# The MLP's gate and up projections in seven block products, with two weight sums made by accumulating transfers

## The chip, the cores and the metric

The kernel runs on one core of a Trainium2 chip. The metric is the device time of one execution, in microseconds (us). A core has five engines that run their own instruction streams in order: TensorE (PE in the profile) multiplies matrices into PSUM, VectorE (DVE) and ScalarE (ACT) work on tiles, GpSimd (POOL) does a little of the same, and SyncE (SP) issues transfers between the chip's memory and SBUF. An instruction that waits holds up everything behind it on its engine.

## The reference

One decoder layer on 512 tokens of width 1024, in float32: two kinds of attention side by side, an output projection added to the input, and then

```
hn = rms_norm(h, norm2_g)
h  = h + (silu(hn @ w_gate) * (hn @ w_up)) @ w_down      # w_gate, w_up: 1024 x 2816, w_down: 2816 x 1024
return rms_norm(h, norm_f_g)
```

## The kernel before

A float32 product is made from three matmuls of rounded halves: each operand is split into hi (a rounded copy, a CAST) and lo (what is left, a subtraction), and `mm3` adds hi·hi, hi·lo and lo·hi into one PSUM bank. So each weight tile that arrives (`w_raw`, 128x512) costs a CAST on ScalarE and a subtraction on VectorE or GpSimd (`split`, which makes `w_hl`) before TensorE can use it.

The work of interest has four stages. Attention ends with `finish_pair`, which puts the last pair's output into `act_hi` on ScalarE and `act_lo` on GpSimd. The second half of the output projection follows (`w_o[f, :, 512:1024]` for f = 0 to 7): the bank is added to the first half's sum (`hp`, kept in memory) to give `h1`, which is scaled and split into `Xh` and `Xl` and turned into `h1t` for the norm. Then gate and up: for each of 22 units j of 128 hidden columns, `gate_up` makes two banks of 128x512 with 8 x 3 matmuls each, and `swiglu` joins them. The norm's factor per token (`R2`) is applied to the results, not to X. Last, down: two passes of 22 steps with four token tiles each, the final norm and the stores.

The instructions of each engine are ordered by a scheduler when the program is built; a buffer that is used again makes the new writer wait for the old readers. The tile pool `ws` that holds `w_raw` and `w_hl` lives through the whole program, while pool `ff`, which takes the space of the attention's pool, opens after attention: its tiles wait until what lay there is no longer used.

Of the kernel before, what the change touches and what calls it, by code (L numbers as in the profile page):

```python
# [16 lines left out]
P = 128  # L17
S = 512
# [20 lines left out]
BUFS = {"w_raw": 3, "w_hl": 5, "pf": 2, "P": 2, "T": 2, "mf": 1, "oc": 1, "g": 4, "h1": 5, "pair": 1}  # L39
ENG = {"0": "apav", "ob": "ap", "s": "vvvp", "w": "avap", "m": "vp", "o0": "av", "b0": "vpvp", "v0": "vv", "r0":  # L40
# [12 lines left out]
def tile_hybrid_layer(ctx: ExitStack, tc: tile.TileContext, xT, w_qk0, w_t, w_av, w_vb, w_o, w_gu, w_d,  # L53
# [5 lines left out]
    ws = ctx.enter_context(tc.tile_pool(name="ws", bufs=2))  # L59
# [27 lines left out]
    def mm3(ps, w, sl, xh, xl, first, last):  # L87

        nc.tensor.matmul(ps, w[:, 0, sl], xh, start=first, stop=False)  # L89
        nc.tensor.matmul(ps, w[:, 0, sl], xl, start=False, stop=False)  # L90
        nc.tensor.matmul(ps, w[:, 1, sl], xh, start=False, stop=last)  # L91
# [47 lines left out]

    ph1 = ExitStack()  # L140
# [161 lines left out]
    mixh = act.tile([P, KT, S], F32R, name="act_hi")  # L302
    mixl = act.tile([P, KT, S], F32R, name="act_lo")
# [73 lines left out]
    def blocks(i, wi, tok):  # L377

        f = scaled(proj_t(i, tok), 1.0, MISC["tr"])
        r = at.tile([P, 2, S], F32, name="Qb", bufs=2)  # L380
        nb = S - CSTRIDE
        for g in range(2):
            gp = slice(64 * g, 64 * g + 64)
            nc.gpsimd.memset(r[64:128, g, nb:], 0.0)
            for h, n in ((0, S), (1, nb)):
                hp = slice(64 * h, 64 * h + 64)
                nc.vector.tensor_tensor(out=r[hp, g, :n].rearrange("p (n l) -> p n l", l=CSTRIDE),
                                        in0=f[gp, S - n:].rearrange("p (n l) -> p n l", l=CSTRIDE), op=ALU.add,
                                        in1=pos_sb[gp, None, h].to_broadcast([64, n // CSTRIDE, CSTRIDE]))
        rhl = (mixh if wi == 0 else mixl)[:, 4:8].rearrange("p (x g) s -> p x g s", x=2)  # L390
# [244 lines left out]


    Gh = [act.tile([P, KT, S], F32R, name=n) for n in ("act_hi", "act_lo")]
    G6 = ff.tile([P, 2 * NJ - 2 * KT, S], F32R, name="G6", bufs=1)
    slots = [Gh[i // KT][:, i % KT] for i in range(2 * KT)] + [G6[:, i] for i in range(2 * NJ - 2 * KT)]
    GH, GL = slots[:NJ], slots[NJ:]  # L640
    TAGS = ("S", "proj", "PT", "S", "proj", "PT", "PT")

    def gate_up(j, a):
        ps = bank(TAGS[(2 * j + a) % len(TAGS)])
        for c in range(2):
            w = split(w_gu[j, a, :, c * WC:(c + 1) * WC], WC, *ENG["gu"][2 * c:2 * c + 2])
            for k in range(4):
                kt = 4 * c + k
                mm3(ps, w, slice(k * P, (k + 1) * P), Xh[:, kt], Xl[:, kt], kt == 0, kt == KT - 1)
        return ps  # L650

    def swiglu(j, pg, pu):
        z = ff.tile([P, S], F32, name="g", bufs=BUFS["g"])
        tt("v", z, pg, R2, ALU.mult)
        nc.scalar.activation(z, z, AF.Silu)
        tt(ENG["h"][0], z, z, R2, ALU.mult)
        tt("v", z, pu, z, ALU.mult)
        copy(ENG["h"][1], GH[j], z)
        tt(ENG["h"][2], GL[j], z, GH[j].bitcast(F32), ALU.subtract)
# [29 lines left out]

    def combine(ps, t, c):  # L690
        tt("v", cell(t, c), ps[t], cell(t, c), ALU.add)
        square(t, c)
        if c == 0:
            tt(ENG["c"], cell(t, 0), cell(t, 0), gf[:, :HD], ALU.mult)
        else:
            finish(t)

    held = None
    for c in range(2):
        ps = [bank(n) for n in (("S", "S", "proj", "proj"), ("PT", "PT", "PT", "O"))[c]]  # L700
        for k in range(NJ - LAST):
            w = w_down(k, c)
            for t in range(NT):
                down(ps, t, k, w)
            if held and k in (1, 3, 5, 7):
                combine(held, k // 2, 0)
        ws_last = [w_down(k, c) for k in range(NJ - LAST, NJ)]
        for t in range(NT):
            for i, k in enumerate(range(NJ - LAST, NJ)):
                down(ps, t, k, ws_last[i])  # L710
            if c == 1:
                combine(ps, t, 1)
        held = ps
# [78 lines left out]
```

## Time and profile before

| | |
|---|---|
| median of 3 runs (lowest to highest) | 682.05 us (680.85 to 682.81) |
| profiled execution, its own time | 679.24 us |
| its span, first to last instruction | 677.5 us |
| mean granted TensorE clock | 0.986 of full speed |
| TensorE matmul busy | 657.1 us (97%) |
| VectorE, ScalarE, GpSimd busy | 381.5, 305.5, 143.8 us |

The time of an execution is its span and 1.7 us around it. A busy time counts an engine's instructions; matmuls overlap each other in the records, so how fast TensorE goes is read from the distance of their starts. "Granted clock" is the share of full TensorE speed (2.4 GHz) that was allowed in a stretch; 0.5 would be the lower level, 1.2 GHz.

### The profile page before, as it was taken

The numbers are of one execution on the slowest core, as the hardware profiler recorded it, in microseconds if no ns is written. First come the engines' busy times: TensorE is split into PE (matmuls) and PEld (weight loads), VectorE is DVE, ScalarE is ACT, GpSimd is POOL, SyncE is SP. The second block draws the span as 40 slices with busy tenths as digits, with TensorE's granted clock in tenths as the row PEclk, the third lists the DMA queues.
The fourth block names the chain that finished last, engine by engine and source line by source line (L and its number), as shares of the span: only waits on it lengthen the run. The fifth ranks groups of instructions, "written<-read, shape, count | busy, mean of one in ns | idle before, by whom it ended". The sixth has DMA issues, their size and how long they took to land.

```text
span 677.5 us, 9409 instructions
## 1 busy us (share of the span) xinstructions
PE 657.1 (97%) x3150; PEld 547.0 (81%) x3150; DVE 381.5 (56%) x828; ACT 305.5 (45%) x668; POOL 143.8 (21%) x184
## 2 busy tenths in 40 slices
PE   9999997999999999899999999999999999999995
PEld 6888897888878887778888888888888888888884
DVE  4468776777877679484645555445445532243225
ACT  5544565436765678466433333333333322232214
POOL 6635842253355455320000000000000000000000
PEclk9999998989999999999999999999999999999998
DMA  6766666445236640062222222222223232213213
GB/s 187 225 172 187 174 171 162 126 138 160 79 110 167 208 121 5 1 228 83 94 94 104 98 94 94 100 103 93 94 94 104 98 124 94 93 66 120 94 48 124
DMA packets 47180, 80.13 MB, mean 118 GB/s; under 512 B 7019, under 2 KB 10347, under 8 KB 47132
## 3 DMA queue, kind: packets, MB, share of 16 engines
q1 hardware_dynamic: 46556, 78.48, 37.2%
q10 hardware_dynamic: 576, 1.05, 0.4%
q8 instruction: 25, 0.41, 0.3%
q14 instruction: 23, 0.19, 0.1%
HBM read 66.36 MB, written 5.55 MB: 106 GB/s over the span
## 4 chain that ended last, share of the span: by engine, by line
PE 92%; DVE 3%; ACT 2%; DMA 1%; issue 1%; SPq 0%; ACTq 0%; DVEq 0%
PE proj L89 9%; PE proj L90 9%; PE proj L91 9%; PE PT L89 5%; PE PT L90 5%; PE PT L91 5%; PE S L89 4%; PE S L90 4%; PE S L91 4%; PE PT L340 3%; PE proj L96 2%; PE proj L95 2%; PE proj L97 2%; PE PT L96 2%; PE PT L95 2%; PE PT L97 2%
## 5 line engine op out<-in xcount | busy, mean ns | idle before, releaser
L71 ACT CAST w_hl<-w_raw 128x512 fp32r<-128x512 f32 (+2 forms) x187 | 112.2, 603 | 261.5 <-PE PT L91 62.9
L84 DVE TENSOR_TENSOR w_hl<-w_raw,w_hl 128x512 fp32r<-128x512 f32 (+1 forms) x169 | 116.9, 693 | 145.1 <-ACT w_hl L71 144.6
L84 POOL TENSOR_TENSOR w_hl<-w_raw,w_hl 128x512 fp32r<-128x512 f32 (+1 forms) x47 | 60.9, 1301 | 63.5 <-ACT w_hl L71 26.1
L337 POOL TENSOR_SCALAR P<-P,den 128x512 f32<-128x512 f32 (+1 forms) x96 | 51.5, 558 | 39.1 <-DVE den L329 27.4
L325 ACT ACTIVATE P<-P,mn 128x512 f32<-128x512 f32 (+1 forms) x96 | 53.5, 559 | 12.7 <-DVE mn L323 12.5
L89 PE MATMUL PT<-Xh,w_hl 128*128 128x512 f32 x144 | 56.0, 389 | 0.0
L90 PE MATMUL PT<-Xl,w_hl 128*128 128x512 f32 x144 | 56.0, 389 | 0.0
L91 PE MATMUL PT<-Xh,w_hl 128*128 128x512 f32 x144 | 56.0, 389 | 0.0
L76 DVE TENSOR_TENSOR PTl<-PT,PTh 128x512 fp32r<-128x512 f32 (+2 forms) x96 | 43.8, 482 | 9.7 <-ACT PTh L350 9.3
L323 DVE CUSTOM_DVE_ANT_0 P<-S,T 128x512 f32<-128x512 f32 (+1 forms) x96 | 44.0, 483 | 8.6 <-PE S L318 7.1
L350 ACT CAST PTh<-PT 128x512 fp32r<-128x512 f32 (+2 forms) x96 | 38.1, 426 | 22.3 <-PE PT L340 18.3
L89 PE MATMUL proj<-xh,w_hl 128*128 128x512 f32 x112 | 45.9, 410 | 0.0
L90 PE MATMUL proj<-xl,w_hl 128*128 128x512 f32 x112 | 45.2, 403 | 0.0
L91 PE MATMUL proj<-xh,w_hl 128*128 128x512 f32 x112 | 45.1, 403 | 0.0
L91 PE MATMUL S<-Xh,w_hl 128*128 128x512 f32 x104 | 40.9, 393 | 0.0
L89 PE MATMUL S<-Xh,w_hl 128*128 128x512 f32 x104 | 40.7, 392 | 0.0
L90 PE MATMUL S<-Xl,w_hl 128*128 128x512 f32 x104 | 40.5, 389 | 0.0
L89 PE MATMUL proj<-Xh,w_hl 128*128 128x512 f32 x104 | 40.5, 389 | 0.0
L90 PE MATMUL proj<-Xl,w_hl 128*128 128x512 f32 x104 | 40.5, 389 | 0.0
L91 PE MATMUL proj<-Xh,w_hl 128*128 128x512 f32 x104 | 40.5, 389 | 0.0
L340 PE MATMUL PT<-ident,P 128*128 128x128 f32 x240 | 36.0, 273 | 0.8 <-POOL P L337 0.8
L340 PEld LDWEIGHTS PT<-ident,P 128*128 128x128 f32 x240 | 28.3, 140 | 5.1 <-POOL P L337 1.3
(275 smaller groups left out, 1423.4 us busy)
## 6 DMA issues: line engine op xcount, KB each, us to landing
w_raw<-in_w_gu_dram SPq DMA_DIRECT2D x88, 256.0 KB, 2.7
w_raw<-in_w_d_dram SPq DMA_DIRECT2D x44, 256.0 KB, 2.8
w_raw<-in_w_t_dram SPq DMA_DIRECT2D x28, 256.0 KB, 2.9
T<-gd SPq DMA_DIRECT2D x64, 64.0 KB, 2.0
w_raw<-in_w_o_dram SPq DMA_DIRECT2D x16, 256.0 KB, 3.0
w_raw<-in_w_vb_dram SPq DMA_DIRECT2D x16, 140.0 KB, 2.2
Qb<-in_xT_dram SPq DMA_DIRECT2D x8, 256.0 KB, 3.0
w_raw<-in_w_av_dram SPq DMA_DIRECT2D x8, 256.0 KB, 2.8
```

The lines of the kernel that those rows point to most:

```text
L71: nc.scalar.copy(out, in_)
L76: engines[e].tensor_tensor(out=out, in0=in0, in1=in1, op=op)
L84: engines[lo].tensor_tensor(out=w[:, 1, :n], in0=raw[:, :n], in1=w[:, 0, :n].bitcast(F32), op=ALU.subtract)
L89: nc.tensor.matmul(ps, w[:, 0, sl], xh, start=first, stop=False)
L90: nc.tensor.matmul(ps, w[:, 0, sl], xl, start=False, stop=False)
L91: nc.tensor.matmul(ps, w[:, 1, sl], xh, start=False, stop=last)
L95: nc.tensor.matmul(ps, xh, w[:, 0, sl], start=first, stop=False)
L323: nc.vector.tensor_tensor_reduce(out=pp, in0=sv, in1=T[:, S - w:], op0=ALU.add, op1=ALU.min, scale=1.0, scalar=3e38, accum_out=mn[:, t:t + 1])
L325: nc.scalar.activation(pp, pp, AF.Exp, bias=mn[:, t:t + 1], scale=-1.0, accum_out=den[:, t:t + 1])
L337: nc.gpsimd.tensor_scalar(pp, pp, den[:, t:t + 1], 1.0, op0=ALU.mult, op1=ALU.mult)
L340: nc.tensor.transpose(pv[:, kb * P:(kb + 1) * P], pp[:, kb * P:(kb + 1) * P], ident)
L350: nc.scalar.copy(ov[0], pv)
```

## The change

The gate and up weights of a unit, cut into first and second 512 inputs, are four blocks: a and b of gate, c and d of up. The tokens are cut into two halves of 256. The eight block products that make the unit's gate and up (each over 512 inputs, 256 tokens) become seven products of sums of blocks: a, b, d, S1 = c + d, S2 = S1 + a, S3 = c + a and S4 = S2 + b, each with its own sum of blocks of X. Each product is 4 x 3 matmuls of 256 columns, so a unit has 84 matmuls of 256 columns where it had 48 of 512. The results are put together with three copies on ScalarE (`q1`, `p5`, `u2`) and adds on VectorE.

Weights are loaded into double tiles (`raw2`, 128x1024, split in one CAST and one subtraction into `hl2`); d has tiles of its own (`raw1`, `hl1`). S1 and S3 are made by transfers: c is loaded by SP, and GpSimd then issues a transfer of d (for S1) or a (for S3) that adds to the same tile. S2 and S4 are additions on VectorE. So seven transfers of 256 KB a unit take the place of four.

X is made in `lower` and `upper`: two blocks of the first 512 inputs (`X1`) and five of the second (`X2`), sums made on VectorE and then split in hi and lo. The output projection's second half takes pairs of f, with loads from pool `ff` (the pool `ws` now closes with attention). z and y of the units stay in float32 and are split in the down stage, which makes one pass with all eight banks; `h1t` goes to memory (`h1d`) and comes back at the end. The act tiles are cut in four.

```
-BUFS = {"w_raw": 3, "w_hl": 5, ..., "g": 4, "h1": 5, "pair": 1}
+BUFS = {"w_raw": 3, "w_hl": 5, ..., "g": 2, "h1": 4, "pair": 1, "raw2": 5, "raw1": 3,
+        "hl2": 3, "hl1": 2, "xe": 2, "xf": 1, "q": 6, "y": 2}
+SUMS = "d"
-ENG = {..., "ob": "ap", ...}
+ENG = {..., "ob": "pvpv", ...}
...
+    def lower(k):
+        e = ff.tile([P, 3, HS], F32, name="xe", bufs=BUFS["xe"])
+        nc.scalar.activation(e[:, 0:3:2], h1s[k].rearrange("p (a n) -> p a n", a=2), AF.Copy, scale=ng[:, k:k + 1])
+        tt("v", e[:, 1], e[:, 0], e[:, 2], ALU.subtract)
+        copy("a", X1[0][:, k], e[:, 0:2])
+        tt("v", X1[1][:, k], e[:, 0:2], X1[0][:, k].bitcast(F32), ALU.subtract)
+        return e
+    def upper(k, e):
+        f = ff.tile([P, 5, HS], F32, name="xf", bufs=BUFS["xf"])
...
+        copy("a", X2[0][:, k], f)
+        tt("v", X2[1][:, k], f, X2[0][:, k].bitcast(F32), ALU.subtract)
+    for k in range(HK):
+        raw = raw2()
+        for n, f in enumerate((k, HK + k)):
+            nc.sync.dma_start(raw[:, n], w_o[f, :, 512:1024])
+        w = split2(raw, "a", ENG["ob"][k])
...
+    def weights(j):
+        l0, l1, l2, d = raw2(), raw2(), raw2(), raw1()
+        nc.sync.dma_start(l0[:, 0], w_gu[j, 0, :, 0:WC])
+        nc.sync.dma_start(d, w_gu[j, 1, :, WC:])
+        nc.sync.dma_start(l1[:, 1], w_gu[j, 0, :, WC:])
+        if SUMS == "d":
+            nc.sync.dma_start(l0[:, 1], w_gu[j, 1, :, 0:WC])
+            nc.gpsimd.dma_start(l0[:, 1], w_gu[j, 1, :, WC:], accum_op=ALU.add)
+            nc.sync.dma_start(l2[:, 1], w_gu[j, 1, :, 0:WC])
+            nc.gpsimd.dma_start(l2[:, 1], w_gu[j, 0, :, 0:WC], accum_op=ALU.add)
...
+        w0 = split2(l0, "a", "v")
+        tt("v", l1[:, 0], l0[:, 1], l0[:, 0], ALU.add)
+        w1 = split2(l1, "a", "v")
+        tt("v", l2[:, 0], l1[:, 0], l1[:, 1], ALU.add)
...
+        w2 = split2(l2, "a", "v")
+        wd = split1(d, "a", "v")
+    def product(ps, w, X, b, first):
+        for k in range(HK):
+            mm3(ps, w, slice(k * P, (k + 1) * P), X[0][:, k, b], X[1][:, k, b], first and k == 0, k == HK - 1, True)
-    for j in range(NJ):
-        pg = gate_up(j, 0)
-        if j == 0:
-            second_norm()
-        pu = gate_up(j, 1)
-        swiglu(j, pg, pu)
+    for j in range(NJ):
+        now = first_part(j)
+        if j == 0:
+            second_norm()
+        else:
+            third_part(j - 1, before)
+        second_part(j, now)
+        before = now
+    third_part(NJ - 1, before)
```

`first_part` does the products a and S1, `second_part` S2, b, S4 and S3, `third_part` d.

How the rows stand on VectorE in the middle of gate and up, before, for about one unit and a half (`w_hl` is a lo, the other rows are `swiglu`):

```order
L76 TENSOR_TENSOR g_4300<-S_4265,g_4300 128x512
L84 TENSOR_TENSOR w_hl_4387<-w_raw_4385,w_hl_4387 128x512
L76 TENSOR_TENSOR G6_3573<-g_4300,act_lo_3572 128x512
L84 TENSOR_TENSOR w_hl_4404<-w_raw_4402,w_hl_4404 128x512
L76 TENSOR_TENSOR g_4377<-proj_4307,R2_3570 128x512
L84 TENSOR_TENSOR w_hl_4422<-w_raw_4420,w_hl_4422 128x512
L76 TENSOR_TENSOR g_4377<-g_4377,R2_3570 128x512
L84 TENSOR_TENSOR w_hl_4439<-w_raw_4437,w_hl_4439 128x512
L76 TENSOR_TENSOR g_4377<-PT_4342,g_4377 128x512
L84 TENSOR_TENSOR w_hl_4464<-w_raw_4462,w_hl_4464 128x512
L76 TENSOR_TENSOR G6_3573<-g_4377,act_lo_3572 128x512
L84 TENSOR_TENSOR w_hl_4481<-w_raw_4479,w_hl_4481 128x512
```

After, one unit's length of VectorE's rows, with the tile numbers: `raw2_4387`, `raw2_4388` and `raw2_4389` are l0, l1 and l2 of unit 6, `raw2_4261`, `raw2_4262`, `raw2_4263` those of unit 5, and `raw2_4136` is l1 of unit 4 (the rows begin with S2 of unit 5; the next row behind them is `raw2_4388<-raw2_4387`, S2 of unit 6):

```order
L77 TENSOR_TENSOR raw2_4262<-raw2_4261 128x512
L77 TENSOR_TENSOR hl1_4157<-raw1_4138,hl1_4157 128x512
L77 TENSOR_TENSOR raw2_4263<-raw2_4262 128x512
L77 TENSOR_TENSOR y_4037<-proj_4036,q_4040 128x256
L77 TENSOR_TENSOR hl2_4150<-raw2_4136,hl2_4150 128x1024
L77 TENSOR_TENSOR y_4037<-y_4037,R2_3594 128x512
L77 TENSOR_TENSOR act00_3595<-S_4034,q_4039 128x256
L77 TENSOR_TENSOR act00_3595<-act00_3595,y_4037 128x256
L77 TENSOR_TENSOR hl2_4154<-raw2_4137,hl2_4154 128x1024
L77 TENSOR_TENSOR y_4163<-PT_4161,q_4164 128x256
L77 TENSOR_TENSOR hl2_4272<-raw2_4261,hl2_4272 128x1024
L77 TENSOR_TENSOR act00_3595<-S_4034,y_4037 128x256
```

A unit's four lo subtractions of 512 have become three of 1024 (`hl2`) and one of 512 (`hl1`), with two sums into `raw2` between them. S2 is the first reader of what the accumulating transfer leaves in l0. The tile `raw2_4387` lies where `raw2_4136` lay (there are five such buffers), whose last reader is the fifth row, `hl2_4150<-raw2_4136`.

The transfers of unit 6 on SP, after (L699 is a, L703 the load of c into l0, L701 b, L705 the load of c into l2, L700 a later unit's d; the first waits for that fifth row):

```order
L699 DMA raw2_4387<-in_w_gu_dram 128x512
L703 DMA raw2_4387<-in_w_gu_dram 128x512
L701 DMA raw2_4388<-in_w_gu_dram 128x512
L705 DMA raw2_4389<-in_w_gu_dram 128x512
L700 DMA raw1_4642<-in_w_gu_dram 128x512
L699 DMA raw2_4513<-in_w_gu_dram 128x512
```

Before, SP had four loads a unit into three buffers `w_raw` here. The accumulating transfers L704 and L706 are not SP's: they stand on GpSimd in pairs, one pair a unit, behind its last subtractions of the output projection, where GpSimd had no row before. Each unit's L704 waits there for the load L703 to have landed, and L706 of a unit stands before L704 of the next.

The other place is the end of the output projection on VectorE, before (`h1` is the sum of bank and `hp`, `Xl` the lo of X, `nv` and `nt` belong to the norm):

```order
L599 SCALAR_TENSOR_TENSOR Xl_3327<-h1_3451,g_sb_78,Xh_3326 128x512
L596 TENSOR_TENSOR h1_3481<-S_3468,g_3461 128x512
L73 COPY h1t_3328<-PT_3485 128x4x128
L84 TENSOR_TENSOR w_hl_3652<-w_raw_3650,w_hl_3652 128x512
L599 SCALAR_TENSOR_TENSOR Xl_3327<-h1_3481,g_sb_78,Xh_3326 128x512
L596 TENSOR_TENSOR h1_3511<-proj_3498,g_3491 128x512
L84 TENSOR_TENSOR w_hl_3669<-w_raw_3667,w_hl_3669 128x512
L599 SCALAR_TENSOR_TENSOR Xl_3327<-h1_3511,g_sb_78,Xh_3326 128x512
L596 TENSOR_TENSOR h1_3541<-S_3528,g_3521 128x512
L73 COPY h1t_3328<-PT_3545 128x4x128
L84 TENSOR_TENSOR w_hl_3694<-w_raw_3692,w_hl_3694 128x512
L599 SCALAR_TENSOR_TENSOR Xl_3327<-h1_3541,g_sb_78,Xh_3326 128x512
```

The same place after (`X21` is the lo of X2, of size 128x1280; `xf` its five blocks):

```order
L77 TENSOR_TENSOR raw2_3885<-raw2_3884 128x512
L676 TENSOR_SCALAR nt_85<-nrstd_t_82,nv_84,nt_85 128x1
L632 SCALAR_TENSOR_TENSOR xf_3562<-xf_3562,xe_3534 128x256
L77 TENSOR_TENSOR xf_3562<-xf_3562,xe_3534 128x256
L675 RECIPROCAL nrstd_t_82<-nt_85 128x1 x2
L677 RECIPROCAL nrstd_t_82<-nt_85 128x1
L635 SCALAR_TENSOR_TENSOR xf_3562<-xf_3562 128x256
L676 TENSOR_SCALAR nt_85<-nrstd_t_82,nv_84,nt_85 128x1 x2
L677 RECIPROCAL nrstd_t_82<-nt_85 128x1 x2
L135 TENSOR_TENSOR g_3695<-ident_66,nrstd_t_82 128x512
L77 TENSOR_TENSOR X21_3332<-xf_3562,X20_3331 128x1280
L77 TENSOR_TENSOR hl2_3772<-raw2_3758,hl2_3772 128x1024
```

The row `X21_3332<-xf_3562` is the last of X2. From the first h1 of the stage to it there are 60 rows, sums of blocks, splits of X and of unit 0's and unit 1's weights, where the old order had h1 and one subtraction `Xl` for each f.

## Rows read from the trace of the kernel before

**Rows 1.** The page, busy time of each engine and the chain that ended last
```profile
PE 657.1 (97%) x3150; PEld 547.0 (81%) x3150; DVE 381.5 (56%) x828; ACT 305.5 (45%) x668; POOL 143.8 (21%) x184
...
PE 92%; DVE 3%; ACT 2%; DMA 1%; issue 1%; SPq 0%; ACTq 0%; DVEq 0%
```

**Rows 2.** By stage: its length; PE, PEld, DVE, ACT, POOL busy; clock, DMA share, GB/s
```profile
286.25:304.78 18.53, 18.20 (x84) 14.75 (x85) 13.71 (x20) 11.52 (x20) 5.08 (x4) 0.91 0.63 207
304.78:546.09 241.31, 241.31 (x1070) 199.52 (x1069) 123.63 (x194) 90.95 (x156) 0.00 (x0) 1.00 0.28 96
546.09:669.40 123.31, 123.29 (x529) 98.89 (x527) 39.30 (x64) 33.37 (x61) 0.00 (x0) 1.00 0.26 90
```

**Rows 3.** Order of time, TensorE in gate and up: start, us, instruction
```profile
399.89 0.39 PE L89 MATMUL S<-Xh,w_hl 128*128 128x512 f32 x1
...
403.97 0.39 PE L89 MATMUL S<-Xh,w_hl 128*128 128x512 f32 x1
```

**Rows 4.** Order of time, TensorE, matmuls of 280 and of 256 columns
```profile
126.02 0.29 PE L97 MATMUL proj<-w_hl,xl 128*128 128x280 f32 x1
...
127.17 0.29 PE L97 MATMUL proj<-w_hl,xl 128*128 128x280 f32 x1
...
128.06 0.28 PE L317 MATMUL S<-KDb,Qb 128*128 128x256 f32 x1
128.18 0.28 PE L318 MATMUL S<-KL,Qb 128*128 128x256 f32 x1
```

**Rows 5.** Groups by form, VectorE: busy us, mean ns, idle before
```profile
L76 DVE TENSOR_TENSOR PTl<-PT,PTh 128x256 fp32r<-128x256 f32 x24 | 10.0, 416 | 0.5 <-ACT PTh L350 0.5
...
L76 DVE TENSOR_TENSOR g<-g,R 128x512 f32<-128x512 f32 x22 | 15.1, 692 | 1.1 <-ACT g L655 1.1
...
L76 DVE TENSOR_TENSOR act_hi<-Qb,act_hi 128x1024 fp32r<-128x1024 f32 x1 | 1.2, 1225 | 0.1
...
L620 DVE TENSOR_SCALAR nt<-rstd_t,nv,nt 128x1 f32<-128x1 f32 x8 | 2.1, 272 | 0.2
```

**Rows 6.** Transfers: SP's issue in ns, from first to last; size and us to landing
```profile
L81 SPq DMA_DIRECT2D w_raw<-in_w_gu_dram x88: 327/328/432, 291.5 to 525.9; - x88
...
L81 SPq DMA_DIRECT2D w_raw<-in_w_o_dram x16: 328/368/866, 138.8 to 243.8; - x16
...
DMA to landing us min/median/max: 2.1/2.8/4.3
...
w_raw<-in_w_o_dram SPq DMA_DIRECT2D x16, 256.0 KB, 3.0
...
Xh<-in_gf_dram SPq DMA_DIRECT2D x1, 512.0 KB, 4.3
```

**Rows 7.** Busy time in windows of 5 us behind attention
```profile
285.00:290.00 5.00, 3.75 (x10) 3.00 (x11) 0.54 (x1) 1.32 (x3) 1.36 (x2) 0.66 0.28 75
290.00:295.00 5.00, 4.67 (x25) 3.63 (x24) 4.33 (x6) 3.71 (x7) 3.72 (x3) 1.00 0.87 296
```

**Rows 8.** Order of time, the end of attention, all engines
```profile
286.25 0.80 PE L89 MATMUL proj<-act_hi,w_hl 128*128 128x512 f32 x1 [2.04 <-ACT act_hi L71]
286.28 1.27 POOL L372 TENSOR_TENSOR act_lo<-mf,act_hi 128x512 fp32r<-128x512 f32 x1 [9.56 <-ACT act_hi L71]
...
287.58 1.76 SPq L589 DMA_DIRECT2D g<-hp  x4
```

**Rows 9.** Chain that ended last, 274 to 280 us: start, us, what
```profile
274.55 0.23 PE S L89
...
279.11 0.23 PE S L91
279.34 0.44 PE PT L340 x4
```

**Rows 10.** Groups by form, ScalarE and GpSimd
```profile
L71 ACT CAST w_hl<-w_raw 128x512 fp32r<-128x512 f32 x171 | 106.1, 621 | 255.0 <-PE PT L91 62.9 <-PE proj L91 50.9 <-PE S L91 40.5
...
L84 POOL TENSOR_TENSOR w_hl<-w_raw,w_hl 128x512 fp32r<-128x512 f32 x39 | 53.5, 1378 | 58.0 <-ACT w_hl L71 20.5 <-DVE w_hl L73 14.1 <-issue 13.1
```

More of the change, by code (lines that the diff above doesn't have):

```diff
@@ L85, in split, with mm3 @@
         return w
[L87 to L91, printed above, removed]
+    def mm3(ps, w, sl, xh, xl, first, last, skip=False):
+        nc.tensor.matmul(ps, w[:, 0, sl], xh, start=first, stop=False, skip_group_check=skip)
+        nc.tensor.matmul(ps, w[:, 0, sl], xl, start=False, stop=False, skip_group_check=skip)
+        nc.tensor.matmul(ps, w[:, 1, sl], xh, start=False, stop=last, skip_group_check=skip)
     def mm3x(ps, xh, xl, w, sl, first, last):
@@ L299, in project_vb @@
             make_vb(t, ps)
-    mixh = act.tile([P, KT, S], F32R, name="act_hi")
-    mixl = act.tile([P, KT, S], F32R, name="act_lo")
+    mix2 = [[act.tile([P, KT // 2, S], F32R, name="act%d%d" % (x, c)) for c in range(2)] for x in range(2)]
+    mixh, mixl = [[m[ft // 4][:, ft % 4] for ft in range(KT)] for m in mix2]
     PO = [0, 128, 384, 768]
@@ new lines, in tile_hybrid_layer @@
+    last = []
+    for k in range(HK):
[3 more added lines that the diff above has]
+        w = split2(raw, "a", ENG["ob"][k])
+        for n, f in enumerate((k, HK + k)):
+            xr = ff.tile([P, S], F32, name="g", bufs=BUFS["g"])
+            nc.sync.dma_start(xr, hp[f * P:(f + 1) * P, :])
+            ps = bank(("proj", "S")[f % 2])
+            for ft in range(4, KT):
+                mm3(ps, w[:, :, n], slice((ft - 4) * P, (ft - 3) * P), mixh[ft], mixl[ft], ft == 4, ft == KT - 1)
+            h1 = ff.tile([P, S], F32, name="h1", bufs=BUFS["h1"])
+            h1s[f] = h1
+            nc.vector.tensor_tensor(out=h1, in0=ps, in1=xr, op=ALU.add)
+            if n == 0:
+                e = lower(k)
+            else:
+                upper(k, e)
+            last.append(f)
+            if len(last) > DELAY:
+                turn(last[len(last) - 1 - DELAY])
@@ new lines, in tile_hybrid_layer, with w_down @@
+    GH = [GT[0][:, k] for k in range(4)] + [GT[2][:, k] for k in range(10)] + [GT[3][:, k] for k in range(8)]
+    GL = [GT[1][:, k] for k in range(4)]
+    gf = [ff.tile([P, HD], F32, name="y", bufs=BUFS["y"]) for _ in range(2)]
+    for c in range(2):
+        nc.sync.dma_start(gf[c], gf_row[:, c * HD:(c + 1) * HD].to_broadcast([P, HD]))
+    def w_down(k):
+        raw = raw2()
+        nc.sync.dma_start(raw, w_d[k * P:(k + 1) * P, :].rearrange("p (a n) -> p a n", a=2))
+        return split2(raw, *ENG["d"])
@@ new lines, in split_g, with down @@
+    def split_g(k):
+        if k % 4 == 0 and k:
+            q = act.tile([P, 4, S], F32R, name=quads[k // 4 - 1]) if k < 20 else GT[3][:, 8:]
+            GL.extend(q[:, i] for i in range(min(4, NJ - k)))
+        copy("a", GH[k], zs[k])
+        tt("v", GL[k], zs[k], GH[k].bitcast(F32), ALU.subtract)
+    def down(ps, t, c, k, w):
+        tk = slice(t * P, (t + 1) * P)
+        mm3x(ps[c][t], GH[k][:, tk], GL[k][:, tk], w[:, :, c], slice(0, HD), k == 0, k == NJ - 1)
+    ps = [[bank(n) for n in ("S", "S", "proj", "proj")], [bank(n) for n in ("PT", "PT", "PT", "O")]]
@@ new lines, in tile_hybrid_layer, with cell @@
+    for k in range(NJ - LAST):
+        w = w_down(k)
+        split_g(k)
+        for c in range(2):
+            for t in range(NT):
+                down(ps, t, c, k, w)
+    h1r = [ff.tile([P, 2, D], F32, name=tag, bufs=1) for tag in ("X10", "X11")]
+    for t in range(NT):
+        nc.sync.dma_start(h1r[t // 2][:, t % 2], h1d[t])
+    def cell(t, c):
+        return h1r[t // 2][:, t % 2, c * HD:(c + 1) * HD]
+    ws_last = []
+    for k in range(NJ - LAST, NJ):
+        ws_last.append(w_down(k))
+        split_g(k)
@@ L682, in finish @@
+    for t in range(NT):
+        for c in range(2):
+            for i, k in enumerate(range(NJ - LAST, NJ)):
+                down(ps, t, c, k, ws_last[i])
+            x = cell(t, c)
+            nc.vector.scalar_tensor_tensor(out=x, in0=ps[c][t], scalar=nrstd_t[:, t:t + 1], in1=x, op0=ALU.mult,
+                                           op1=ALU.add)
+            square(t, c, x)
+            if c == 0:
+                tt(ENG["c"], x, x, gf[0], ALU.mult)
+        rsqrt(t, rstd_t)
         r = rstd_t[:, t:t + 1]
@@ L688, in finish @@
         nc.scalar.dma_start(out[t * P:(t + 1) * P, :HD], x)
[L690 to L713, printed above, removed]
 def _bucket(dist):
```

159 lines of the change are left out of this document (92 added, 67 removed).

## The prediction

> **What bounds the kernel now.** I read the page first: TensorE is busy 97% of the span and holds 92% of the chain that ended last [rows 1]. Then the stages. In gate and up, 241.31 us long, TensorE is busy throughout at clock 1.00, VectorE 123.63 and ScalarE 90.95 us of it, GpSimd nothing; so columns on TensorE are the bound there, and VectorE has half its time free. In the output projection's second half before it, 18.53 us long, VectorE is busy 13.71 us: there it is nearly as full as TensorE. Down is TensorE's again [rows 2]. Third, the order of time gives TensorE's own pace: 18 matmuls of 512 columns from 399.89 to 403.97, 0.2267 us each [rows 3].
>
> **Columns saved.** Nine matmuls of 280 columns start 0.128 us apart, two of 256 columns 0.120 [rows 4]. A unit was 48 x 0.2267 = 10.88 us and is 84 x 0.120 = 10.08 us, 0.80 less, 17.6 us over 22 units. The line through 512 and 280 columns gives 0.1178 for 256; 0.120 is read directly and I take it.
>
> **VectorE and ScalarE in gate and up.** Durations on VectorE: 0.416 us for 256 columns, 0.692 for 512, 1.225 for 1024 [rows 5]; 256 more columns cost about 0.27, so 1280 is about 1.49. A unit's rows (three lo of 1024, one of 512, two sums, the scaling by R2, five adds or products of 256) come to 3 x 1.225 + 4 x 0.692 + 5 x 0.416 = 8.5 us. That lies beside TensorE's 10.08 only if VectorE is never held up; 1.5 us of cover is left where there were 5. ScalarE's casts are at most 3 x 1.24 + 0.62 [rows 10], and with three copies and a Silu they stay near 6 us: covered. GpSimd gets two transfers a unit and nothing else.
>
> **The loop through the accumulating transfer.** This is the added wait. VectorE's row `hl2_4150` (lo of l1, unit 4) frees the buffer of unit 6's l0. Then SP issues a and c one behind the other (an issue takes 0.33, c starts about 0.4 later), c lands, GpSimd issues the adding transfer of d, and when that has landed, VectorE's S2 of unit 6 can run. VectorE works in order: behind S2 stand `hl1`, the next sum, a y of 256 and the lo that frees the next unit's buffer, and behind those the adds that empty TensorE's banks. S2 to that lo is 3 x 0.692 + 0.416 + 1.225 = 3.7 us. c lands 3.0 us from its issue, as the pairs of w_o did [rows 6]. With 0.1 for two semaphores, one turn of the loop is 3.7 + 0.4 + 3.0 + 0.1 + A = 7.2 + A, where A is the adding transfer from issue to landing. One turn is one unit. TensorE sets the pace while A is under 2.9 us; beyond that every unit costs 7.2 + A, and A above 3.7 eats the 0.80 saved.
>
> A is in no row. From below: a plain load of that size, 2.8 at the median (the lowest of all is 2.1), since it brings the same 256 KB. From above: the load and a pass over the destination one behind the other, 5.6. Between them: 256 KB more at the 296 GB/s of the fullest window [rows 7] is 0.9, so 3.7; the one load of 512 KB took 4.3 [rows 6]. The transfer handles 256 KB of source and 256 KB of what lies there, which is nearest to these two; I take 4.0 between them. Then a unit is 11.2 us, 1.12 above TensorE's 10.08.
>
> No row shows a transfer issued by GpSimd. The Trainium skill, "DMA: Bandwidth & Descriptors", section "Latency and other measured facts", puts the first byte about 0.4 us later from GpSimd's queue than from SP's: A would be 4.4 and the sum 8.4 us more (an estimate from that page).
>
> **The way into gate and up.** Before, the last w_o load was issued at 243.8, long ahead [rows 6], so matmuls of the second half filled TensorE inside attention: 18 of the L89 to L91 rows stand on the chain from 274.55 to 279.34 [rows 9]. Now w_o comes into pool `ff`, which opens when attention's last reader, `act_lo` on GpSimd, is done; SP's loads of hp show that wait at 287.58, when act_lo (286.28, 1.27 long) has ended [rows 8]. Without the 18 fillers attention ends 18 x 0.2267 = 4.1 us sooner, at 283.5. Then a pair of loads lands (0.4 + 3.0) at 286.9, the cast (1.24) ends at 288.1, GpSimd's lo of 1024 (two of 512: 1.27 each as in [rows 8], 1.38 in the mean [rows 10]) at 290.7. TensorE starts at 288.1 where it started at 286.25, and has all 96 matmuls ahead. VectorE's first h1 comes at about 293.0.
>
> From there VectorE has 60 rows to the last lo of X2: 4 of 1280, 5 of 1024, 23 of 512, 16 of 256 and 12 small ones (at most 0.27, [rows 5]): 6.0 + 6.1 + 15.9 + 6.7 + 3.2 = 37.9 us, so X2 is whole at 331.0. TensorE would need 96 x 0.2267 = 21.8, eight turns of four (0.44 each, [rows 9]) 3.5, 75 matmuls of gate and up that want no X2's end 9.0, and 2.0 for the clock (0.66 in the window of 285 to 290, where TensorE had waited, [rows 7]): 324.4. So it waits 6.6 us for VectorE. Then the other 1773 matmuls, 212.8 us, and once more 2.0 for the clock: 545.8, where gate and up ended at 546.09 [rows 2]. So the saving of 17.6 us is spent on the way in, and the change without the loop is worth 0.3 us. If VectorE's rows there have gaps, each microsecond adds one.
>
> **Down and the end.** The 528 matmuls of down are the same; a step's splits on VectorE (1.225 + 0.692) lie beside 24 x 0.2267 = 5.44 us of TensorE. h1t goes to memory and back in time that transfers leave free (DMA share 0.26 to 0.28, [rows 2]). I cost these at nothing; without that cover the four loads of h1t would cost one landing, about 4 us.
>
> **The sum.** 679.24 - 0.3 + 21 units (1773 / 84) x 1.12 = 702.4 for the profiled execution. The median of the runs is 2.8 us above that execution, so 705.
>
> **Rivals.** First, the other side: TensorE sets the pace. That is decided at A = 2.9, at the S2 row: if the adding transfer lands like a plain load (2.8, the median of [rows 6]), the loop closes in 10.0 us and each unit runs at TensorE's pace. Then the time is 682 with 0.120 per matmul; with 0.1178 it is 1773 x 0.0022 = 3.9 us less, 678. For it: a share of only 0.28 of the DMA engines is used in this stage, so bandwidth isn't short. Against it: the transfer also reads what it adds to. Half of this case is faster, half no change.
>
> Second, heavier: the passes of the adding transfer follow each other, A = 5.6, a unit 12.8, 21 x 2.72 = 57 more, 739.
>
> Third, VectorE keeps GpSimd from issuing. GpSimd's 512 subtraction took 1.27 while VectorE was quiet [rows 8] and 1.38 in the mean [rows 10], a slight sign of the two disturbing each other. If an issue waited for one lo row of VectorE, 1.2, a unit would be 12.4 and the time 21 x 1.2 = 25 above the forecast, 730. The Trainium skill, "SBUF — State Buffer", section "Who interferes with whom", says that a DMA from GpSimd starves while VectorE holds their shared ports, and that a VectorE instruction with two SBUF inputs contends with GpSimd's reads; by the first, this rival would bite, by the second mostly not, since nearly all rows of VectorE here are of that kind. No row of before has a GpSimd transfer beside VectorE.
>
> I leave out that 256 columns don't cover a weight load: at 280 columns TensorE kept 0.128 us, near the line from 512 [rows 4].
>
> **How the numbers follow.** Forecast, A of 3.2 to 4.9: 688 to 724, chance 0.56. First rival 0.24 (678 to 682). Second and third 0.20 (730 to 739). The range reaches from 677 to 737; outside it I leave less than 0.2, the top of the second rival and a way in that costs other than worked out. A change within 0.3% (680 to 684) can't be told from none: faster 0.13, same 0.11, slower 0.76.
>
> **What the changed profile would show.** Right: VectorE's S2 (raw2 from raw2) waits in every unit for a transfer into raw2; units about 11.2 us apart, TensorE idle about 1 us in each; L704 landing in about 4; TensorE idle about 6 us before X2's last lo, and VectorE without gaps from 293 to 331; down 123 us long. Wrong: units 10.1 apart and TensorE full (first rival), L704 landing above 5 or GpSimd long in issuing it (second, third), VectorE waiting for other things than l0 in the loop, or attention not ending sooner than before.

## The result: 754.91 us, and the profile after

The changed kernel takes 754.91 us at the median, where the kernel before took 681.45 (679.42 to 682.81) on the same chip: ratio 1.107, 95% interval 1.103 to 1.112. Three of its four executions took 753.18 to 755.86 us; the fourth, a slow one at a mean granted clock of 0.741 (0.95 in the others), took 825.0 and counts in the median alone. The forecast was 705 with a range from 677 to 737: the direction was right, the size not, and the time lies outside the range. The profiled execution took 755.86 us, its span 754.0.

The page after, with busy times, the chain that ended last, and the transfers of the gate and up weights (size, median us from issue to landing), beside [rows 1, 6]:

```profile
PE 666.4 (88%) x3942; PEld 588.9 (78%) x3942; DVE 449.5 (60%) x935; ACT 345.8 (46%) x716; POOL 176.6 (23%) x222
...
PE 18%; issue 9%; DVE 6%; DMA 5%; SPq 0%; ACT 0%; DVEq 0%; POOLq 0%; ACTq 0%
...
raw<-in_w_gu_dram SPq DMA_DIRECT2D x110, 256.0 KB, 3.4
raw<-in_w_gu_dram POOLq DMA_DIRECT2D x44, 256.0 KB, 4.6
```

TensorE has 792 more matmuls, yet only 9 us more busy time. The chain can be followed back only to 450.8 us here, the last 40% of the span; in that part TensorE holds 18 points and issue, VectorE and transfers 20, where TensorE held 92 of 100 before. The stages, cut where the blocks of X were whole (340.2), gate and up ended (620.9) and down's last matmul ended (739.9); columns as in [rows 2]:

```profile
340.20:620.90 280.70, 240.33 (x1811) 234.01 (x1810) 167.31 (x259) 111.21 (x178) 32.81 (x38) 0.93 0.56 140
620.90:739.90 119.00, 115.79 (x494) 92.01 (x493) 37.86 (x44) 31.53 (x44) 0.00 (x0) 1.00 0.24 82
739.90:754.00 14.10, 0.00 (x0) 0.00 (x0) 8.91 (x28) 7.34 (x19) 0.00 (x0) 0.66 0.40 149
```

In gate and up TensorE has gaps (240.33 busy of 280.70) and a mean clock of 0.93, where it was full at 1.00 [rows 2]; no other engine is near its length. So the time is spent in waits. The group of TensorE's rows with the longest idle time ahead of them (busy us, mean ns, idle us before and what ended it) is the lo·hi matmul of product b, which waits for VectorE's lo of l1:

```profile
L92 PE MATMUL PT<-X,hl 128*128 128x256 f32 x88 | 30.2, 343 | 38.7 <-DVE hl L77 38.7
```

That lo stands on VectorE behind the next unit's S2 (the fifth row of the order shown above, S2 being the first). One unit shows what S2 waits for. The order of time, one unit of gate and up, a few rows of VectorE, SP, GpSimd:

```profile
430.90 1.22 DVE L77 TENSOR_TENSOR hl<-raw,hl 128x1024 fp32r<-128x1024 f32 x1
...
432.15 0.33 SPq L699 DMA_DIRECT2D raw<-in_w_gu_dram  x1
...
432.53 0.42 SPq L703 DMA_DIRECT2D raw<-in_w_gu_dram  x1
...
436.64 0.86 POOL L704 DMA_DIRECT2D raw<-in_w_gu_dram  x1 [6.37 <-DMA raw<-in_w_gu_dram]
...
442.18 0.69 DVE L77 TENSOR_TENSOR raw<-raw 128x512 f32<-128x512 f32 x1 [4.77 <-issue]
...
444.33 1.22 DVE L77 TENSOR_TENSOR hl<-raw,hl 128x1024 fp32r<-128x1024 f32 x1
...
445.57 0.33 SPq L699 DMA_DIRECT2D raw<-in_w_gu_dram  x1
```

Here the loop of the prediction can be read link by link. VectorE's lo ends at 432.12 and frees the buffer; SP issues a (432.15) and c (432.53); c has landed and GpSimd issues the adding transfer at 436.64; VectorE, idle for 4.77 us, begins S2 at 442.18; its next lo frees the next buffer, and SP starts again at 445.57, 13.42 us after it started before. The view names "issue" and no transfer as what VectorE waited for: it doesn't always find a landing that fits, so the wait must be followed by hand through GpSimd's row.

Sixteen units lie between these two S2 rows (of VectorE's order of time), 13.42 us each in the mean (12.0 to 14.2):

```profile
374.87 0.69 DVE L77 TENSOR_TENSOR raw<-raw 128x512 f32<-128x512 f32 x1 [4.94 <-issue]
...
589.56 0.69 DVE L77 TENSOR_TENSOR raw<-raw 128x512 f32<-128x512 f32 x1 [4.68 <-issue]
```

From c's issue to the start of GpSimd's instruction it is 4.43 us in the mean of sixteen units, from there to S2 5.24, from S2 to c's next issue 3.77; the sum is 13.44. The landing of the adding transfers, L704 (which makes S1) and L706 (which makes S3) by themselves (lengths of the issue in ns; min, median, max to landing):

```profile
L704 POOL DMA_DIRECT2D raw<-in_w_gu_dram x22: 862/862/1022, 300.6 to 584.2; - x22
...
DMA to landing us min/median/max: 3.9/5.2/7.3
...
L706 POOL DMA_DIRECT2D raw<-in_w_gu_dram x22: 862/862/875, 304.0 to 589.0; - x22
...
DMA to landing us min/median/max: 3.5/4.1/7.1
```

Both add, and both move the same bytes; only L704 stands in the loop, and it lands 1.1 us later. In the unit above the load of b goes out 1.0 us ahead of L704 (435.61) and the second load of c 0.5 behind it (437.10).

### The profile page after: what moved, and what is told of

Same layout as the page of the kernel before. It is cut to its first block, busy times and chain, and to the rows that moved or that the text cites. A ratio compares the mean times of both kernels' runs of the same rounds, so it can differ in the third digit from the quotient of the medians.

```text
span 754.0 us, 11222 instructions
## 1 busy us (share of the span) xinstructions
PE 666.4 (88%) x3942; PEld 588.9 (78%) x3942; DVE 449.5 (60%) x935; ACT 345.8 (46%) x716; POOL 176.6 (23%) x222
## 5 line engine op out<-in xcount | busy, mean ns | idle before, releaser
L77 DVE TENSOR_TENSOR hl<-raw,hl 128x1024 fp32r<-128x1024 f32 (+1 forms) x112 | 124.9, 1117 | 99.1 <-ACT hl L72 94.6
L72 ACT CAST hl<-raw 128x1024 fp32r<-128x1024 f32 (+1 forms) x114 | 109.1, 966 | 109.7 <-PE O L98 74.9
L91 PE MATMUL S<-X,hl 128*128 128x256 f32 x352 | 103.7, 297 | 3.0 <-DVE X L77 3.0
L90 PE MATMUL S<-X,hl 128*128 128x256 f32 x352 | 102.3, 299 | 2.0 <-ACT q L739 1.2
L92 PE MATMUL S<-X,hl 128*128 128x256 f32 x352 | 103.1, 295 | 0.0
L77 DVE TENSOR_TENSOR raw<-raw 128x512 f32<-128x512 f32 x44 | 30.3, 688 | 89.6 <-issue 80.2
L91 PEld LDWEIGHTS S<-X,hl 128*128 128x128 f32 x352 | 72.6, 206 | 3.3 <-DVE X L77 3.2
L90 PEld LDWEIGHTS S<-X,hl 128*128 128x128 f32 x352 | 71.8, 208 | 3.0 <-ACT q L739 1.5
L92 PEld LDWEIGHTS S<-X,hl 128*128 128x128 f32 x352 | 72.2, 205 | 0.0
L92 PE MATMUL PT<-X,hl 128*128 128x256 f32 x88 | 30.2, 343 | 38.7 <-DVE hl L77 38.7
L704 POOL DMA_DIRECT2D raw<-in_w_gu_dram x22 | 19.1, 870 | 148.7 <-DMA raw<-in_w_gu_dram 108.8
L92 PEld LDWEIGHTS PT<-X,hl 128*128 128x128 f32 x88 | 19.9, 226 | 42.1 <-DVE hl L77 42.1
L92 PE MATMUL proj<-X,hl 128*128 128x256 f32 x176 | 50.0, 284 | 1.4 <-DVE hl L77 1.4
L91 PE MATMUL proj<-X,hl 128*128 128x256 f32 x176 | 50.1, 285 | 0.0
L90 PE MATMUL proj<-X,hl 128*128 128x256 f32 x176 | 50.0, 284 | 0.0
L77 DVE TENSOR_TENSOR PTl<-PT,PTh 128x256 fp32r<-128x256 f32 (+2 forms) x96 | 44.2, 482 | 6.3 <-ACT PTh L353 5.9
L353 ACT CAST PTh<-PT 128x256 fp32r<-128x256 f32 (+2 forms) x96 | 37.7, 424 | 17.4 <-PE PT L343 12.6
```

The source lines that it names most:

```text
L72: nc.scalar.copy(out, in_)
L77: engines[e].tensor_tensor(out=out, in0=in0, in1=in1, op=op)
L353: nc.scalar.copy(ov[0], pv)
```

## The experiments

Unless said otherwise an edit is made to the changed kernel. Ratios are to the kernel before, run on the same chip.

**The form of the sums.** Both sums on VectorE, with no adding transfer at all:

```
-SUMS = "d"
+SUMS = "v"
```

> Both weight sums of a unit are made by VectorE (c is loaded into a tile of its own, two additions of 512 columns, 0.69 us each), and no transfer adds. Loop theory (a unit takes 13.4 us because VectorE's S2 waits for buffer, load of c and adding transfer one behind the other): the adding transfer's 5.2 us go from the loop, which then closes in 8 to 9 us, so TensorE's 10.1 or VectorE's 8.5 + 1.4 = 9.9 us set the unit, and the time is 755 - 21 x 3.3 = 686, at most 695 where VectorE's rows don't fit into TensorE's gaps. Rival, five or more loads of 256 KB a unit are what takes 13.4 us: five loads remain of seven transfers, so a unit of 10 to 13 us. Rival, the way in and the end hold the loss: above 740.

693.48 us, ratio 1.019 (1.016 to 1.021): 61 us come back, and in the steady part a unit takes 9.9 to 10.0 us. So the adding transfers carried the loss, and not the way in alone; 12 us stay that they don't explain.

**What in the transfer is long.** The same transfers without the addition (this kernel leaves the two sums out, so it does not compute the layer):

```
-nc.gpsimd.dma_start(l0[:, 1], w_gu[j, 1, :, WC:], accum_op=ALU.add)
+nc.gpsimd.dma_start(l0[:, 1], w_gu[j, 1, :, WC:])
-nc.gpsimd.dma_start(l2[:, 1], w_gu[j, 0, :, 0:WC], accum_op=ALU.add)
+nc.gpsimd.dma_start(l2[:, 1], w_gu[j, 0, :, 0:WC])
```

> The two transfers that GpSimd issues write d and a over c and add nothing, so S1 is d alone and S3 is a alone: the sums are left out. Every instruction stands where it stood on every engine. If reading and adding what lies there is what makes the transfer long, it lands in about 3.5 us (a plain load from SP took 2.8 to 3.4) in place of 5.2 and a unit is 11.7 us: 755 - 21 x 1.7 = 719 (712 to 728). If the length is that of a transfer from GpSimd's queue whatever it does: 750 or more.

724.94 us, ratio 1.065 (1.062 to 1.069). The same view of L704 as above, without the addition:

```profile
L704 POOL DMA_DIRECT2D raw<-in_w_gu_dram x22: 536/536/737, 297.2 to 555.1; - x22
...
DMA to landing us min/median/max: 3.0/3.9/4.8
```

The median landing falls from 5.2 to 3.9 us (L706's from 4.1 to 3.1), GpSimd's issue from 862 to 536 ns, and the mean from GpSimd's start to S2 from 5.24 to 3.72. A unit is 11.96 us, 1.46 less, and 21 x 1.46 = 31 us is the 30 that the time lost. Each 0.1 us of the transfer is 2 us of the kernel: the transfer stands in the loop whole. The addition is 1.5 us of it; of the rest, 0.8 us is what L704 lands later than L706 in the same run, though neither adds there.

**The order of VectorE.** Every transfer, sum and size as changed; only S2 may not stand ahead of the preceding unit's lo of l1, which `split2` puts into the list `held`:

```
+with tc.issue_after(held[-1].ins) if held else ExitStack():
     tt("v", l1[:, 0], l0[:, 1], l0[:, 0], ALU.add)
-w1 = split2(l1, "a", "v")
+w1 = split2(l1, "a", "v", held)
```

> S2 of a unit is kept behind the lo of the preceding unit's l1 on VectorE, some four rows later than the scheduler put it; all transfers, sums and sizes stay. Then two units pass in one turn of the loop. Loop theory: (9.8 us from a freed buffer to the sum, and about 9 us of rows) / 2 is under 10.1, TensorE sets the pace, VectorE no longer idles ahead of S2, and the time is 755 - 21 x 3.3 = 686 (680 to 696). Rival, the transfers' rate (two adding transfers and five loads in 13.4 us) or GpSimd held up by VectorE: no change beyond 10 us, 745 to 757.

694.36 us, ratio 1.020 (1.018 to 1.023), the same as with the sums on VectorE. 180 us of gate and up, columns as in [rows 2]:

```profile
360.00:540.00 180.00, 179.09 (x1515) 178.60 (x1514) 139.98 (x218) 90.75 (x144) 30.23 (x35) 1.00 0.72 182
```

TensorE is full again (179.09 of 180), at clock 1.00, with the DMA share at 0.72 where it was 0.56: the transfers weren't at their limit, nor was GpSimd. VectorE's idle time ahead of its sums went from 89.6 to 11.2 us in all, in these rows of the groups, of the changed kernel and of this one:

```profile
L77 DVE TENSOR_TENSOR raw<-raw 128x512 f32<-128x512 f32 x44 | 30.3, 688 | 89.6 <-issue 80.2 <-DMA raw<-in_w_gu_dram 9.4
```

```profile
L77 DVE TENSOR_TENSOR raw<-raw 128x512 f32<-128x512 f32 x44 | 30.2, 686 | 11.2 <-issue 9.1 <-DVE hl L77 2.1
```

A landing of the adding transfer of 5.0 us at the median (4.0 to 6.6) hurts no more when two units pass in a turn of the loop. This decides between the theories: it was latency in an order, not a rate.

**More buffers.** Six, and eight:

```
-"raw2": 5
+"raw2": 6
...
-"raw2": 5
+"raw2": 8
```

> raw2 has six buffers in place of five, nothing else. With six, unit 7's l0 takes the place of unit 5's l0, and the scheduler puts S2 of unit 7 ahead of the row that frees the next one: from S2 to that lo stand S2, a y of 256 and the lo of 1024, 2.3 us in place of 3.7. Loop theory: a unit is 13.4 - 1.4 = 12.0 us, the time 755 - 21 x 1.4 = 726 (718 to 734). Rival, the latency is hidden by any deeper prefetch: TensorE's pace, 685 to 695. Rival, the adding transfers themselves need 13.4 us a unit (their rate, or GpSimd): no change, 750 to 757.

> The changed kernel as it is, with eight raw2 buffers in place of five (24 KB in place of 12 KB ahead). The scheduler then puts S2 of a unit three buffers further ahead too, so that on VectorE there stand, as with five, S2, three rows of 0.4 to 0.7 and the lo of 1024 from S2 to the row that frees the next l0. Loop theory: 3.7 + 9.7 us a unit again, 750 to 757. Rival, latency that deeper buffers hide: 686 to 700. Both know the six buffers' 730.

Six: 729.58 us, ratio 1.072 (1.067 to 1.077), a unit 11.8. Eight: 752.81 us, ratio 1.106 (1.102 to 1.111), a unit 13.2; VectorE idles 76.7 us ahead of the sums. So eight buffers are no better than five, and worse than six. With more buffers the order that the scheduler makes has S2 further ahead as well; what counts in these three kernels is which rows of VectorE stand from S2 to the lo that frees the next buffer (2.3 us of them with six, 3.7 with five and eight).

**The end.** From here on the edits add up, each made to the kernel before it, beginning with the one with S2 put later. TensorE's last matmul is followed by 14.1 us where it was 8.1 [rows 2 give down's end, 669.40 of 677.5].

```
-LAST = 4
+LAST = 3
```

> The kernel with S2 put later (694 us), and LAST is 3 in place of 4: three of down's steps are held back for the end, as many as hl2 has buffers. With four, the fourth step's weights wait for a buffer, all eight banks end in the last 24 matmuls, and VectorE joins eight of them after TensorE's last matmul: 14.1 us to the end where it was 8.1 before. Theory, the end costs 6.0 us that the prediction held for nothing: 688 (686 to 690). Rival, these eight joins are hidden or the end is set by h1t's way back from memory: 693 to 695.

688.11 us, ratio 1.010 (1.007 to 1.013): 6.2 us less. Down holds its last steps back so that the eight banks end one after the other. With four such steps and three `hl2` buffers the fourth's weights come late, and the eight banks end in the last few us, together. VectorE's first joins (X from a bank), in the order of time, of the changed kernel and of this one, where down's last matmul ends at 739.8 and 678.0:

```profile
736.59 0.75 DVE L821 SCALAR_TENSOR_TENSOR X<-S,nrstd_t,X 128x512 f32<-128x512 f32 x1 [1.43 <-PE S L98]
```

```profile
668.66 0.75 DVE L826 SCALAR_TENSOR_TENSOR X<-S,nrstd_t,X 128x512 f32<-128x512 f32 x1 [5.16 <-PE S L98]
```

They begin 3.2 us ahead of the end, and 9.3 with three steps.

**The way in.** Two buffers for `xf`, so that one k's blocks needn't wait for the one before:

```
-"xf": 1
+"xf": 2
```

> The kernel of three last steps, and xf (the float32 blocks of X2's making) has two buffers in place of one. Theory, X2 comes late because each k of upper waits for the one before (8.5 to 10 us from one X2 lo to the next, with about 5 us of work): X2 is whole 2 to 6 us sooner and the time 2 to 5 us shorter, 683 to 686. Rival, VectorE's and ScalarE's rows are full there (9 to 10 of 10 us in some windows): no change, 687 to 690.

690.24 us, ratio 1.013 (1.009 to 1.016): no gain. X2 is whole 3.7 us sooner (334.1, not 337.8), as the theory had it, but gate and up end 3.8 us later (562.8, not 559.0): from 340 to 360 TensorE is busy 15.8 us where it was 19.4. Then the first two pairs of w_o early, ahead of the pools' close, in the buffers that the kernel before used:

```
+for f, tag in ((0, "proj"), (KT // 2, "proj"), (1, "S"), (KT // 2 + 1, "S")):
+    w = split(w_o[f, :, 512:1024], 512, "a", "p")
+    ps = bank(tag)
...
```

> The kernel of two xf, and the first four of w_o's second halves are loaded and split in pool ws before attention ends, as the kernel before did; TensorE can run 36 of their 48 matmuls inside attention. Theory, attention's end is not made by these fillers (it stood at 287.6 with and without them): they are won whole, first h1 comes about 10 us sooner than 299, and the time is 8 to 11 us shorter, 674 to 678. Rival, as the prediction held: each filler makes attention 0.23 us longer, 36 x 0.23 = 8.3 us, and only the waiting for the loads is won: 681 to 685.

685.31 us, ratio 1.006 (1.003 to 1.008): 4.9 less than with two xf, about half of what was expected. `act_lo` on GpSimd, the end of attention, in the order of time, of the changed kernel and of this one:

```profile
286.34 1.26 POOL L375 TENSOR_TENSOR act<-mf,act 128x512 fp32r<-128x512 f32 x1 [7.51 <-ACT act L72]
```

```profile
287.69 1.28 POOL L375 TENSOR_TENSOR act<-mf,act 128x512 fp32r<-128x512 f32 x1 [9.56 <-ACT act L72]
```

One pair of rows says little here: in the eight profiled kernels without fillers this row starts at 282.9 to 286.3 (mean 284.8), in the five with the 36 fillers at 287.1 to 288.1 (mean 287.7). So the fillers make attention about 2.9 us longer, 0.08 us each, far less than their 0.23. But SP's loads behind the early matmuls now wait until the last of these has ended (291.2), and the first w_o load among them goes out at 292.1, not 287.6.

**The start of down.** In the kernel above TensorE waits behind gate and up for ScalarE's and VectorE's splits of a step's weights. The waits of TensorE from 540 us on (us, times, longest):

```profile
PE S L97 <- DVE hl L77: 1.6, 1, 1.6
PE S L96 <- ACT hl L72: 1.5, 1, 1.5
```

The edit keeps step k's rounding behind that of its weights (the list `casts`):

```
+with tc.issue_after(casts[-1].ins) if k > 5 else ExitStack():
     copy("a", GH[k], zs[k])
```

> The kernel with early w_o (685 us), and on ScalarE the rounding of down's left operand for step 6 and on is kept behind the rounding of that step's weights; the scheduler had put twelve of them in one row ahead of the weights, and TensorE waits 3.1 us in the ten us behind gate and up's last product. Theory, these waits go: 682 to 683. Rival, TensorE waits for X2 to be read for the last time, whatever ScalarE's order: 685.

679.24 us, ratio 0.998 (0.996 to 0.9996): 6 us less, twice what was expected. TensorE has no such wait left (20.00 busy of 20 from 560 to 580), and down is 3.7 us shorter in the profile (115.3, not 118.9), about the 3.1 expected. The other 2.7 us lie ahead of gate and up's end (553.7, not 556.4), where the edit changes nothing; their cause was not looked for. This is the one version below the kernel before, by 0.2%, with an interval that ends at 0.9996, the best of twelve edited kernels; it is hardly more than a tie.

Three further edits to it did not help. The norm's squares behind the last rounding of X2 on ScalarE (the list `hi`):

```
+with tc.issue_after(hi[-1].ins):
     for t in range(NT):
...
```

> The kernel before this one, and the eight squares of the norm stand on ScalarE behind the last rounding of X2, not ahead of it. TensorE waits 3.4 us for that rounding. Theory, X2 is whole 3 us sooner and the time is 2 to 3 us shorter, 679 to 681. Rival, the norm's R2 comes later and holds up y of unit 0 and with it the banks: 682 to 685.

682.16 us, ratio 1.001 (0.999 to 1.003): no gain, as the rival had it. TensorE's wait of 3.4 us for the rounding falls to 0.5, and 2.6 us of waits for the adds into z on VectorE come in its place. With X1's lo on GpSimd besides:

```
-tt("v", X1[1][:, k], e[:, 0:2], X1[0][:, k].bitcast(F32), ALU.subtract)
+tt("p", X1[1][:, k], e[:, 0:2], X1[0][:, k].bitcast(F32), ALU.subtract)
```

> The kernel before this one, and GpSimd makes the lo of X1 (four subtractions of 512, 0.68 us each on VectorE, about 1.3 on GpSimd). Theory, VectorE is the bound on the way in: 2 to 3 us shorter, 677 to 679. Rival, ScalarE and the loads bound it, or GpSimd's slower rows hold up the adding transfers behind them: no change or 1 to 3 us longer.

684.04 us, ratio 1.004 (1.002 to 1.006): taking these rows off VectorE gains nothing. Whether ScalarE, the loads or GpSimd's slower rows (1.43 us at the median) bind instead was not separated. And the kernel of down's order with its sums on VectorE (`SUMS = "v"`):

> The kernel of the new down order (679 us) with both weight sums of a unit on VectorE and no adding transfer, five loads a unit in place of seven transfers. With S2 put later the adding transfers no longer set the unit (9.9 us in both forms), so if the theory is right the form of the sums decides nothing any more: 677 to 682. Rival, the transfers hold up the loads on the way in (their share is 0.8 to 1.06 from 290 to 310): 673 to 677. Rival, 1.4 us more of VectorE's rows a unit take the last cover: 682 to 690.

681.46 us, ratio 1.001 (0.999 to 1.002), a unit 9.93 us: once the order has slack, the form of the sums hardly matters.

## Why the prediction was wrong

**The mechanism held.** VectorE's S2 waits in each of the seventeen units from 374.87 to 589.56, the loop is the one that was described, link for link, and the two edits that open it (S2 later, both sums on VectorE) give 60 and 61 us back.

**The term that failed is "21 units x 1.12".** The loop was put at 7.2 + A = 11.2 us and is 13.42. The transfer that adds was priced at 4.0, between a 256 KB load with 0.9 more and the one 512 KB load [rows 6, 7]; it takes 5.24, near the upper bound of 5.6 (load and a pass over the destination one behind the other), which stood as second rival at 739. The addition itself was hardly mispriced (1.2 over a plain load's 2.8; it measured 1.0 to 1.5), and L706, which adds as well, lands in 4.1. The other 1.1 us go with L704's place in the unit, beside the loads of b and of the second c; that these loads cause it is likely and was not tested. The load of c was priced at 3.0 with 0.05 to GpSimd's start and takes 4.43: its landing is 3.7 at the median, where w_o's loads took 3.0, and GpSimd starts 0.55 us or more behind it. In the loop a is issued 0.38 us ahead of c; whether that makes c late was not tested either. The rows from S2 on were priced at 4.1 with SP's issue and are 3.77. Together 21 x 2.22 = 47 us, of which 42 show in the stage, 280.7 us long where 238.3 followed from the prediction's numbers; its first units are paced by X2, not by the loop.

The Trainium skill, "DMA: Bandwidth & Descriptors", section "Latency and other measured facts", has the first byte from GpSimd's queue about 0.4 us behind that from SP's. No run here shows the first byte. Whole landings don't show the difference: without the addition all of GpSimd's transfers landed in 3.3 us at the median and all of SP's gate and up loads in 3.4. The 4.4 that the prediction estimated from that page would have made the unit 11.6, still 1.8 short, and c's link alone was 1.4 too low.

**X2 came 9.2 us late.** These four rows (order of time: SP's first w_o loads, the first rounding, the first h1, X2's last lo) stand against 283.5, 286.9, 293.0 and 331.0 less 1.5:

```profile
287.62 0.83 SPq L644 DMA_DIRECT2D raw<-in_w_o_dram  x2
...
292.50 1.04 ACT L72 CAST hl<-raw 128x1024 fp32r<-128x1024 f32 x1 [6.24 <-DMA g<-hp]
...
299.18 0.69 DVE L654 TENSOR_TENSOR h<-proj,g 128x512 f32<-128x512 f32 x1 [1.74 <-PE proj L92]
...
338.72 1.49 DVE L77 TENSOR_TENSOR X<-xf,X 128x1280 fp32r<-128x1280 f32 x1
```

The first step that failed is "attention ends 18 x 0.2267 = 4.1 us sooner": in this execution it ended at the same time, and in the eight kernels without fillers 1.5 us sooner in the mean (3.4 at most). TensorE has gaps there without the fillers (8.10 busy of the ten us from 270, where it was full), so most of what was taken out left idle time: that the chain ran through TensorE's rows did not mean that taking them out would shorten it by their length. The loads then took 1.5 us more than one pair's landing; the eight w_o loads went out within 5 us and landed in 5.3 us at the median, where w_o's loads took 3.0 before [rows 6]. From the first h1 to X2's end it was 41.0 us against 37.9. VectorE was busy for 33.7 of them and idle for 7.4, where the prediction had no gaps; the longest waits stand ahead of the weight sums of the first units (3.6 us) and of the h1 sums, for TensorE (1.9).

**Down's end was costed at nothing and cost 6.0 us**, the work that hides it having been named for the splits and not for the eight joins. Down itself was 119.0 us against 123.3: some of its matmuls had run in gate and up's waits.

**The sum.** 9.2 + 42.4 - 4.3 + 6.0 = 53.3 us is the distance between the predicted span (700.7) and that of the profile (754.0).

**Right, and unused.** TensorE's saving is real: with the loop open a unit takes 9.93 us, 84 x 0.118, the line through 512 and 280 columns rather than the 0.120 that was taken [rows 4]. Over 22 units that is 21 us, and the changed kernel would spend all of it, loop or no loop, in the way in, the start of down and the end. The first rival's price of 678 to 682, against 694 measured with the loop open, was off for the way in and the end, as the forecast was.

**The other rivals and the chances.** The third rival, VectorE's rows holding up GpSimd's issues, is not borne out by the trace of the changed kernel: of 27 adding transfers for which the landing of c is on record and GpSimd was free, 24 start 0.53 to 0.62 us behind it and three 0.70 to 0.85. Where VectorE is idle throughout that stretch it is 0.55 to 0.70 (seven of them), where it is busy throughout 0.53 to 0.62, and the issue takes 862 ns either way.

The chances don't fit together: 0.56, 0.24 and 0.20 make 1.00 and leave nothing for a time outside the range, which was given "less than 0.2"; and the second rival's 739 lies above the range's own top of 737. The sign set down for the second and third rival, L704 landing above 5, did come.

## What to carry to other kernels

A buffer that is freed, loaded, added to and read again is a loop, and its length divided by the units that pass in one turn is a floor on the time of a unit. Where the loop passes through an engine that works in order, the number of units per turn is set by where the reader stands in that order, and more buffers can leave it as it was (eight here); the cheapest remedy here was to move one reader behind one row.

Both transfers of the loop were priced from rows of other stages, and both came out too low, by 1.2 and 1.4 us. The same kind of transfer landed 1.1 us apart at two places of one unit, so such a link is priced with the transfers that the loop itself has under way, and the time from a landing to the next issue (0.55 us here) is part of it. And a saving on the bound engine pays only if the stages at both ends are not lengthened by what makes it possible.

## What the runs showed of the hardware

A 256 KB transfer that adds, issued by GpSimd, landed in 5.2 us at the median (L704, 3.9 to 7.3) or 4.1 (L706, 3.5 to 7.1) and occupied GpSimd for 0.86 us; without the addition the landings were 3.9 (3.0 to 4.8) and 3.1 (3.0 to 5.4), and the issue 0.54. With S2 put later, where the units follow each other in 9.9 us, both landed in 5.0.

TensorE's clock fell behind a wait, and not at once. In the changed kernel TensorE stood still for 3.13 us until 592.98, ran at the upper level (2.4 GHz, matmuls of 256 columns 0.118 us apart) for about 1.2 us, then at the lower one (1.2 GHz, 0.213 apart) for 3.4 us, and then at the upper one again. Windows of TensorE in that unit, columns as in [rows 2]:

```profile
590.00:592.90 2.90, 0.00 (x0) 0.00 (x0) 2.90 (x6) 0.00 (x0) 0.00 (x0) 1.00 0.55 90
593.00:594.10 1.10, 1.10 (x9) 1.10 (x10) 0.86 (x2) 0.54 (x2) 0.00 (x0) 1.00 0.34 45
594.20:597.50 3.30, 3.30 (x17) 3.30 (x17) 2.77 (x4) 2.77 (x5) 0.00 (x0) 0.50 0.45 148
597.60:600.00 2.40, 2.40 (x22) 2.40 (x22) 1.21 (x3) 1.34 (x3) 0.00 (x0) 1.00 0.79 258
```

With the waits gone the clock is 1.00 (the kernel with S2 put later, above). The loop's length shows no trace of it: its three links are those of VectorE, SP and GpSimd.
